# A decoder layer's 64 experts on one core: w1 stored beside w3, two rounding parts in one matmul, blocks of 64 tokens, other groups of tokens

## The chip, the cores and the metric

The kernel runs on one core of a Trainium2 chip. The metric is the device time of one execution in microseconds (us). Before the change it was 3769.25 us, the median of three runs (3760.1 to 3776.89 us).

## What is computed

The reference is one layer of a decoder: a token mixer (RWKV-7, indexer-selected sparse attention and sliding-window attention side by side), then a mixture of experts (MoE). The change touches the second part only. There, 2048 tokens of 1024 numbers are each sent to 8 of 64 experts, and to one shared expert of the same shape:

```python
def swiglu(t, w1, w3, w2):
    return (jax.nn.silu(t @ w1) * (t @ w3)) @ w2
...
    out = grouped_experts(t, idx, gate, w1, w3, w2) + swiglu(t, sw1, sw3, sw2)
```

w1 and w3 are 1024 x 256 and w2 is 256 x 1024, in float32. A token's result is the sum of its 8 experts' outputs, each times the gate of the token for that expert, plus the shared expert's output. A layer norm of that sum with the stream ends the layer.

## The kernel before, in words

**The precision.** TensorE multiplies numbers rounded to its 32-bit matmul type (F32R). To come near float32, each operand is split into a high part (the rounded number) and a low part (the rest), and a product takes three matmuls: high x high, high x low, low x high (`TERMS`, L2017). Every matmul of the experts thus stands three times in the code, and every operand has two tiles. ScalarE (ACT) makes the high part and VectorE (DVE) the low part by a subtraction, for the weights at L1998 and L1999 and for the rest in `split_to` (L58, ACT L61 and DVE L64).

**The units of work.** The experts are ranked by how many tokens chose them; `CAPS` (L1594) has the token capacity of each rank, from 640 down to 128. `group_cuts` (L1603) cuts a capacity into groups of at most 320 tokens. The MoE phase (`moe_phase`, L1953) is a list of units in a fixed order (L2173 to L2181): three units of the shared expert, then the groups of all ranks in the order 0, 63, 1, 62, ..., then the shared expert's other tokens with the last layer norm. There are 82 routed units with 157 blocks of tokens. Their sizes before are 128 or less (21 units), 192 (7), 208 (9), 224 (7), 240 (2), 256 (22), 272 (4), 288 (4), 304 (2) and 320 (4).

**One unit.** `gather` (L2070) fetches the rows of its tokens from memory by indirect DMA on the GpSimd (POOL) queue, one DMA for a block of 128 tokens or what is left. `turn` (L2082) transposes them on TensorE (L2011), eight transposes a block, into the tiles hH and hL. `hidden` (L2019) multiplies by w1 and w3. A unit of more than 128 tokens takes the weights as the stationary operand: for each half m of the 256 hidden columns and for each of w1 and w3 there are 24 matmuls (8 slices k of the 1024 input numbers x 3 terms) of n columns each (L2051), 96 in all. The four sums lie in PSUM tiles of the pool p13, which has three buffers. After each m, silu (ACT L2056), the product (DVE L2057) and a split make gH and gL. A unit of 128 tokens or less takes the tokens as the stationary operand, 48 matmuls of 256 columns (L2032). `back` (L2060) multiplies by w2: for a block and each half of the 1024 output columns six matmuls of 512 columns (L2066), whatever the block's size. `routed` (L2097) scales a result by the gate on ACT (L2102) and adds it to the sums in memory by an indirect DMA (L2103).

**What sets the order.** TensorE's order is written out in the last loop (L2330 to L2371): `hidden` of a unit yields between its matmuls, and `interleave` (L2310) places there the transposes of the next unit and the `back` blocks of the unit before. The rows of tokens are fetched two units ahead, and so are an expert's weights (`matrices`, L2220). A weight goes through four staging buffers of 512 KB (`wraw`, pool wr) on the SP queue, then through ACT L1998 and DVE L1999 into the pool ws. ws has ten tiles and an expert takes six (high and low of w1, w3 and w2), so that a new weight waits until TensorE is done with an old one. The numbers of the tokens (`tokens`, L2124) need a small comparison on DVE (L2119) and a matmul (L2131) first. ACT, DVE, POOL and SP each run their instructions in one fixed order.

Of the kernel before, what the change touches and what calls it, by code (L numbers as in the profile page):

```python
# [13 lines left out]
ALU = mybir.AluOpType  # L14
# [1938 lines left out]
def moe_phase(tc, A, g, S, modrow, out):  # L1953
    nc = tc.nc
    V, G, ACT, PE = nc.vector, nc.gpsimd, nc.scalar, nc.tensor
    with ExitStack() as es:
# [29 lines left out]
        def weights(srcs, into=None, scaled=False):  # L1986

            res = []
            for s in srcs:
                a, b = s.shape[1:]  # L1990
                wh, wl = into or [ws.tile([P, 2048], F32R, name="w") for _ in range(2)]
                for i in range(2):
                    raw = wr.tile([P, 1024], F32, name="wraw")
                    last = nc.sync.dma_start(raw.rearrange("p (a b) -> p a b", b=b), s[:, i * a // 2:(i + 1) * a // 2, :])
                    c = slice(i * 1024, (i + 1) * 1024)
                    if scaled and s is srcs[-1]:
                        V.tensor_tensor(raw, raw, g2b, op=ALU.mult)
                    ACT.activation(wh[:, c], raw, AF.Copy)  # L1998
                    V.tensor_tensor(wl[:, c], raw, wh[:, c].bitcast(F32), op=ALU.subtract)  # L1999
                res.append(tuple(x.rearrange("p (a b) -> p a b", a=a) for x in (wh, wl)))  # L2000
            return res, last

        def expert_matrices(e):
            d = lambda a: a[0][bass.ds(e, 1)].rearrange("o a b -> (o a) b")
            return w13(d(A["exp_w1"])), w13(d(A["exp_w3"])), w2_(d(A["exp_w2"]))
# [13 lines left out]
        def hidden(w, h, n, g_):  # L2019


            hH, hL = h
            gH = gp.tile([P, 2, GMAX], F32R, name="gH")
            gL = gp.tile([P, 2, GMAX], F32R, name="gL")
            g_ += [gH, gL]
            if n <= P:
                ps = []
                for i in range(2):
                    ps.append(p13.tile([P, CH], F32, name="p13"))
                    for k in range(KT):  # L2030
                        for j, (a, b) in enumerate(TERMS):
                            PE.matmul(ps[i][:n, 0:256], lhsT=(hH, hL)[a][:, k, 0:n], rhs=w[i][b][:, k, :],  # L2032
                                      start=(k == 0 and j == 0), stop=(k == KT - 1 and j == 2))
                        if k % STEP == STEP - 1 and (i, k) != (1, KT - 1):
                            yield (2 - i) * (KT // STEP) - k // STEP
                s = gp.tile([P, GMAX], F32, name="s")
                ACT.activation(s[:n, 0:256], ps[0][:n, 0:256], AF.Silu)
                V.tensor_tensor(s[:n, 0:256], s[:n, 0:256], ps[1][:n, 0:256], op=ALU.mult)
# [4 lines left out]
                split_to(nc, gH[:, :, 0:n], gL[:, :, 0:n], pt[:, 0:2 * n].rearrange("p (m t) -> p m t", m=2))  # L2043
                return
            for m in range(2):
                ps = []
                for i in range(2):
                    ps.append(p13.tile([P, CH], F32, name="p13"))
                    for k in range(KT):
                        for j, (a, b) in enumerate(TERMS):  # L2050
                            PE.matmul(ps[i][:, 0:n], lhsT=w[i][a][:, k, m * P:(m + 1) * P], rhs=(hH, hL)[b][:, k, 0:n],  # L2051
                                      start=(k == 0 and j == 0), stop=(k == KT - 1 and j == 2))
# [3 lines left out]
                ACT.activation(s[:, 0:n], ps[0][:, 0:n], AF.Silu)  # L2056
                V.tensor_tensor(s[:, 0:n], s[:, 0:n], ps[1][:, 0:n], op=ALU.mult)  # L2057
                split_to(nc, gH[:, m, 0:n], gL[:, m, 0:n], s[:, 0:n])

        def back(w, gH, gL, c, n):  # L2060
# [355 lines left out]
```

## Time and profile before

| | before |
|---|---|
| median of 3 runs | 3769.25 us |
| the profiled execution's own time | 3762.49 us |
| its span, first to last instruction | 3760.8 us |
| mean granted TensorE clock | 0.964 of full speed |
| experts' stage, routed units with their neighbours | about 2133 to 3630 us of the span |

Views name a group of instructions by line, engine and tile. PE is TensorE's matmuls, PEld its weight loads, which overlap the matmuls. Matmuls overlap in the pipeline, so the time from one start to the next says more than the duration of one. In the chain of waits a piece such as "2.77 PE py L2066 x12" is twelve matmuls that followed each other without a gap, in 2.77 us. "issue" is time for which the profile shows no releaser.

### The profile page before, as it was taken

What the parts mean: (1) busy time and instruction counts of PE and PEld (TensorE: products, weight loads), DVE (VectorE), ACT (ScalarE), POOL (GpSimd) and SP (SyncE); (2) the same over time, 40 slices, a digit from 0 to 9 for tenths busy, and PEclk for the clock granted to TensorE, in tenths of its full rate; (3) what the DMA queues carried; (4) which work ended last, traced back from release to release, by engine and by line L of the source; (5) the groups of instructions that cost most, each with busy time, mean ns of one, the idle gap of its engine ahead of it and who ended that gap; (6) DMA issues with size and microseconds to landing.
All of it is one profiled execution on the core that took longest, in us unless ns stands there. A gap on an engine that the chain in (4) does not pass through costs nothing. (4 is left out here: it accounts for less than half of the span.)

```text
span 3760.8 us, 64004 instructions
## 1 busy us (share of the span) xinstructions
PE 3433.5 (91%) x23044; PEld 2984.6 (79%) x23044; DVE 2670.9 (71%) x7039; ACT 1941.9 (52%) x3439; POOL 883.3 (23%) x817
## 2 busy tenths in 40 slices
PE   7799999799999878999897899999999999999994
PEld 5577777688888767778786799888899888888983
DVE  6556899888888678888799555555665555665669
ACT  4233656355555567766322355555565555556630
POOL 1000000322223255543000122233233223232200
PEclk9899999899999889999998899999999999999997
DMA  7657466400000132222543488888899888888973
GB/s 253 210 192 242 141 216 221 164 27 21 24 24 18 30 107 81 78 69 80 172 149 129 163 213 218 234 237 233 246 266 252 242 223 235 241 248 254 295 226 138
DMA packets 276234, 640.37 MB, mean 170 GB/s; under 512 B 34428, under 2 KB 115364, under 8 KB 275784
## 3 DMA queue, kind: packets, MB, share of 16 engines
q1 hardware_dynamic: 231760, 481.09, 38.1%
q0 software_dynamic: 40832, 150.32, 18.1%
q10 hardware_dynamic: 3320, 4.83, 0.4%
q8 instruction: 182, 2.98, 0.3%
q14 instruction: 140, 1.15, 0.1%
HBM read 467.14 MB, written 169.00 MB: 169 GB/s over the span
## 5 line engine op out<-in xcount | busy, mean ns | idle before, releaser
L2051 PE MATMUL p<-hH,w 128*128 128x256 f32 (+8 forms) x4352 | 872.2, 288 | 9.3 <-DVE w L1999 6.6
L2051 PEld LDWEIGHTS p<-hH,w 128*128 128x128 f32 x4352 | 706.0, 191 | 18.8 <-DVE w L1999 6.9
L1999 DVE TENSOR_TENSOR w<-wraw,w 128x1024 fp32r<-128x1024 f32 x396 | 474.8, 1223 | 285.7 <-ACT w L1998 268.9
L2051 PE MATMUL p<-hL,w 128*128 128x256 f32 (+8 forms) x2176 | 615.9, 283 | 0.7 <-DVE hL L64 0.7
L1998 ACT ACTIVATE w<-wraw 128x1024 fp32r<-128x1024 f32 x396 | 406.1, 1053 | 232.0 <-DMA wraw<-in_exp_w_dram 102.0
L2066 PE MATMUL py<-w,gH 128*128 128x512 f32 (+5 forms) x1384 | 443.8, 403 | 26.2 <-DVE w L2297 14.6
L2103 POOL DMA_INDIRECT scratch_acc<-y,idx x157 | 263.9, 1681 | 797.5 <-ACT y L2102 245.8
L2051 PEld LDWEIGHTS p<-hL,w 128*128 128x128 f32 x2176 | 415.9, 191 | 6.2 <-DVE hL L64 0.9
L285 PE MATMUL pj<-hTH,w 128*128 128x512 f32 x1152 | 379.1, 404 | 21.5 <-ACT w L201 16.4
L64 DVE TENSOR_TENSOR hL<-tr,hH 128x512 fp32r<-128x512 f32 (+7 forms) x346 | 213.0, 626 | 210.9 <-ACT hH L61 192.7
L2066 PEld LDWEIGHTS py<-w,gH 128*128 128x128 f32 (+5 forms) x1384 | 240.5, 182 | 86.7 <-DVE w L2297 15.8
L2102 ACT ACTIVATE y<-py,gt 128x512 f32<-128x512 f32 (+5 forms) x314 | 213.9, 683 | 147.3 <-PE py L2066 131.3
L285 PEld LDWEIGHTS pj<-hTH,w 128*128 128x128 f32 x1152 | 221.9, 194 | 76.0 <-ACT w L201 20.4
L61 ACT ACTIVATE hH<-tr 128x512 fp32r<-128x512 f32 (+7 forms) x346 | 184.0, 544 | 189.6 <-PE tr L2011 165.4
L2066 PE MATMUL py<-w,gL 128*128 128x512 f32 (+5 forms) x692 | 275.9, 399 | 0.3 <-DVE gL L64 0.3
L2077 POOL DMA_INDIRECT x<-scratch_h,idx x157 | 163.5, 1041 | 309.9 <-DVE L L2119 68.5
L285 PE MATMUL pj<-hTL,w 128*128 128x512 f32 x576 | 231.2, 401 | 0.0
L2011 PE MATMUL tr<-ident,x 128*128 128x128 f32 (+5 forms) x1384 | 192.2, 266 | 31.5 <-issue 20.7
L2011 PEld LDWEIGHTS tr<-ident,x 128*128 128x128 f32 (+5 forms) x1384 | 149.8, 141 | 42.7 <-issue 26.0
L2066 PEld LDWEIGHTS py<-w,gL 128*128 128x128 f32 (+5 forms) x692 | 125.2, 181 | 40.0 <-DVE gL L64 1.7
L2032 PE MATMUL p<-w,hH 128*128 128x256 f32 (+2 forms) x736 | 142.6, 291 | 10.7 <-DVE s L2057 10.7
L61 ACT ACTIVATE gH<-s 128x256 fp32r<-128x256 f32 (+8 forms) x136 | 55.1, 405 | 160.4 <-DVE s L2057 147.8
(610 smaller groups left out, 8199.9 us busy)
## 6 DMA issues: line engine op xcount, KB each, us to landing
wraw<-in_exp_w_dram SPq DMA_DIRECT2D x384, 512.0 KB
w<-scratch_wH SPq DMA_DIRECT2D x57, 512.0 KB
w<-scratch_wL SPq DMA_DIRECT2D x57, 512.0 KB
mw<-in_w_mod_dram SPq DMA_DIRECT2D x48, 512.0 KB
scratch_rw<-po SPq DMA_DIRECT2D x44, 256.0 KB
w<-in_w_in_dram SPq DMA_DIRECT2D x21, 512.0 KB
x<-in_x_dram SPq DMA_DIRECT2D x40, 256.0 KB
scratch_wH<-w SPq DMA_DIRECT2D x19, 512.0 KB
```

The source lines that it names most:

```text
L61: nc.scalar.activation(hi, src, AF.Copy)
L64: (lo_eng or nc.vector).tensor_tensor(lo, src, hi.bitcast(F32), op=ALU.subtract)
L285: nc.tensor.matmul(ps, lhsT=a_[:, k, :], rhs=b_[k], start=(k == 0 and i == 0), stop=(k == KT - 1 and i == 2))
L1998: ACT.activation(wh[:, c], raw, AF.Copy)
L1999: V.tensor_tensor(wl[:, c], raw, wh[:, c].bitcast(F32), op=ALU.subtract)
L2011: PE.transpose(ps[:, k * n:(k + 1) * n], x[0:n, (4 * h + k) * P:(4 * h + k + 1) * P], g.ident[0:n, 0:n])
L2032: PE.matmul(ps[i][:n, 0:256], lhsT=(hH, hL)[a][:, k, 0:n], rhs=w[i][b][:, k, :], start=(k == 0 and j == 0), stop=(k == KT - 1 and j == 2))
L2051: PE.matmul(ps[i][:, 0:n], lhsT=w[i][a][:, k, m * P:(m + 1) * P], rhs=(hH, hL)[b][:, k, 0:n], start=(k == 0 and j == 0), stop=(k == KT - 1 ...
L2066: PE.matmul(ps[:n], lhsT=(gH, gL)[a][:, m, c:c + n], rhs=w[2][b][:, m, h * CH:(h + 1) * CH], start=(m == 0 and j == 0), stop=(m == 1 and j ...
L2077: G.indirect_dma_start(out=x[0:m, :], out_offset=None, in_=S["h2"], in_offset=bass.IndirectOffsetOnAxis(ap=ix[0:m], axis=0))
L2102: ACT.activation(y[:m, hs], ps[:m], AF.Copy, scale=gt[:m])
L2103: G.indirect_dma_start(out=S["acc"], out_offset=bass.IndirectOffsetOnAxis(ap=ix[0:m], axis=0), in_=y[0:m, :], in_offset=None, compute_op=A ...
```

## The change

Weights: the two tiles w1 and w3 (high and low of each) become two tiles of another cut. The first holds slices k = 0 to 3 of w1 and of w3 side by side, the second k = 4 to 7. Loads, splits and buffers keep their numbers and sizes, and come in the order w1, w3 of the first tile, w1, w3 of the second.

Units of 128 tokens or less: w1 and w3 go through one matmul of 512 columns, 24 instead of 48 of 256.

Units of 144 to 240 tokens: the tokens' high and low parts lie in one tile hb, and one matmul of 2n columns multiplies both by the high weight; one of n columns adds the low weight. 64 matmuls instead of 96; the two halves of the sum are added afterwards on DVE and ACT.

Blocks: a unit whose last block would have 16 to 64 tokens ends in a block of 64, and the one before is made shorter. In `back` the two parts of 64 tokens make one stationary operand of 128 columns: four matmuls of 512 columns for each output half instead of six. The two halves are added on DVE after a copy on ACT, and the gate is multiplied by a DVE instruction of its own.

Groups: `group_cuts` cuts capacities over 320 in other places. There are still 82 routed units and 157 blocks: 128 tokens (25 units), 192 (6), 208 (2), 224 (8), 240 (6), 256 (17), 272 (5), 288 (6), 304 (3), 320 (4). 24 blocks have 64 tokens.

```diff
@@ group_cuts
     if n <= GMAX:
         return [(0, n)]
-    a = 256
-    if n - a < 192 and 384 < n < 448:
+    if n <= GMAX + P:
+        a = n - P
+    elif n <= 2 * GMAX - 64:
         a = 16 * ((n // 2 + 15) // 16)
+    else:
+        a = 256
     return [(0, a)] + [(a + x, a + y) for x, y in group_cuts(n - a)]
+def blocks_of(n):
+    k, r = divmod(n, P)
+    if k and 0 < r <= 64:
+        cuts = [P] * (k - 1) + [64 + r, 64]
+    else:
+        cuts = [P] * k + [r] * (r > 0)
+    return [(sum(cuts[:i]), m) for i, m in enumerate(cuts)]
...
+        def three(w1, w3, w2, scaled):
+            side = lambda i: lambda t: t.rearrange("p (k i n) -> p k i n", k=4, i=2)[:, :, i, :]
+            half = lambda i: lambda t: t[:, i * 1024:(i + 1) * 1024].rearrange("p (a b) -> p a b", a=1)
+            both = [([(w[:, 4 * q:4 * q + 4, :], side(i)) for i, w in enumerate((w1, w3))], False) for q in range(2)]
+            return both + [([(w2[:, i:i + 1, :], half(i)) for i in range(2)], scaled)]
+        k_of = lambda w, part, k: w[k // 4][part][:, (k % 4) * CH:(k % 4 + 1) * CH]
...
@@ hidden
+            gb = gp.tile([P, 2, 2, 256], F32R, name="gb")
+            gq = gp.tile([P, 2, 2, 64], F32R, name="gq")
+            c, nq = blocks_of(n)[-1]
+            parts = [(gb, 0, c), (gq, c, n)] if nq == 64 and n > P else [(gb, 0, n)]
...
+                ps = p13.tile([P, CH], F32, name="p13")
+                for k in range(KT):
+                    for j, (a, b) in enumerate(TERMS):
+                        PE.matmul(ps[:n], lhsT=hb[:, k, a, 0:n], rhs=k_of(w, b, k),
+                                  start=(k == 0 and j == 0), stop=(k == KT - 1 and j == 2))
...
+            wide = 2 * n <= CH - 32
...
+                        if wide:
+                            two = [(ps[i][:, 0:2 * n].rearrange("p (a t) -> p a t", a=2), wk(0), hb[:, k, :, 0:n]),
+                                   (ps[i][:, 0:n], wk(1), hb[:, k, 0, 0:n])]
+                            for j, (o, l, r) in enumerate(two if k == 0 else two[::-1]):
+                                PE.matmul(o, lhsT=l, rhs=r, start=(k == 0 and j == 0), stop=(k == KT - 1 and j == 1))
...
+                if wide:
+                    s3 = gp.tile([P, 256], F32, name="s3", bufs=1)
+                    V.tensor_copy(s[:, 0:n], ps[0][:, n:2 * n])
+                    V.tensor_tensor(s[:, 0:n], ps[0][:, 0:n], s[:, 0:n], op=ALU.add)
+                    ACT.activation(s3[:, 0:n], ps[1][:, n:2 * n], AF.Copy)
+                    V.tensor_tensor(s3[:, 0:n], ps[1][:, 0:n], s3[:, 0:n], op=ALU.add)
+                    ACT.activation(s[:, 0:n], s[:, 0:n], AF.Silu)
+                    V.tensor_tensor(s[:, 0:n], s[:, 0:n], s3[:, 0:n], op=ALU.mult)
...
-                split_to(nc, gH[:, m, 0:n], gL[:, m, 0:n], s[:, 0:n])
+                for t, a, e in parts:
+                    split_to(nc, t[:, m, 0, 0:e - a], t[:, m, 1, 0:e - a], s[:, a:e])
@@ back
+                    if n == 64:
+                        gq = g_[1][:, m]
+                        two = [(ps, gq.rearrange("p a t -> p (a t)"), w2(0)), (ps[:n], gq[:, 0], w2(1))]
+                        for j, (o, l, r) in enumerate(two if m == 0 else two[::-1]):
+                            PE.matmul(o, lhsT=l, rhs=r, start=(m == 0 and j == 0), stop=(m == 1 and j == 1))
@@ routed
+                    if m == 64:
+                        ACT.activation(y[:m, hs], ps[64:128], AF.Copy)
+                        V.tensor_tensor(y[:m, hs], ps[:m], y[:m, hs], op=ALU.add)
+                    else:
+                        ACT.activation(y[:m, hs], ps[:m], AF.Copy, scale=gt[:m])
+                if m == 64:
+                    V.tensor_scalar(y[:m], y[:m], gt[:m], None, op0=ALU.mult)
```

## Rows read from the trace of the kernel before

**Rows 1.** The page: busy time by engine, and lines of the chain that ended last.

```profile
PE 3433.5 (91%) x23044; PEld 2984.6 (79%) x23044; DVE 2670.9 (71%) x7039; ACT 1941.9 (52%) x3439; POOL 883.3 (23%) x817
...
PE p L2051 18%; PE py L2066 11%; PE tr L2011 3%; PE p L2032 3%; DMA wraw<-in_exp_w_dram 2%; DVE w L1999 1%; ACT w L1998 1%; DVE w L2273 0%; DVE w L2272 0%; DVE lnst L2262 0%; DVE w L2283 0%; DMA scratch_acc<-y,idx 0%; DVE w L2297 0%; DVE hL L64 0%; DVE x L2282 0%
```

**Rows 2.** Busy time in windows of the experts' stage, with clock, DMA share, GB/s.

```profile
2133.00:3630.00 1497.00, 1452.69 (x10444) 1330.45 (x10443) 857.62 (x1931) 840.01 (x1316) 423.44 (x310) 0.99 0.87 243
...
2700.00:2900.00 200.00, 198.11 (x1473) 185.19 (x1472) 122.70 (x287) 116.68 (x182) 63.24 (x44) 1.00 0.91 259
2900.00:3450.00 550.00, 529.24 (x3647) 472.95 (x3647) 320.44 (x735) 313.38 (x492) 161.95 (x121) 0.99 0.86 240
3450.00:3630.00 180.00, 176.06 (x1280) 165.67 (x1279) 104.94 (x189) 99.68 (x155) 40.87 (x29) 0.99 0.94 277
```

**Rows 3.** Waits of TensorE's weight loads, 2120 to 3640: total us, times, longest.

```profile
PEld tr L2011 <- issue: 26.0, 21, 3.4
PEld L2131 <- DVE L L2119: 9.2, 8, 1.3
```

**Rows 4.** The same waits, 2900 to 3450.

```profile
PEld tr L2011 <- issue: 21.1, 17, 3.4
```

**Rows 5.** Chain pieces (start, us, count): columns 192, 224, 256, 272, 288, 304, 320, 512.

```profile
2937.93 1.32 PE p L2051 x12
...
3213.44 1.33 PE p L2051 x12
...
3473.27 1.43 PE p L2051 x12
...
3375.45 3.01 PE p L2051 x24
...
3202.20 3.16 PE p L2051 x24
...
3108.38 3.32 PE p L2051 x24
...
2971.22 3.52 PE p L2051 x24
...
2941.01 2.77 PE py L2066 x12
```

**Rows 6.** DVE and ACT groups, 2120 to 3760: busy, mean ns, idle before and releaser.

```profile
L1999 DVE TENSOR_TENSOR w<-wraw,w 128x1024 fp32r<-128x1024 f32 x386 | 463.0, 1223 | 279.5 <-ACT w L1998 262.7 <-issue 12.0 <-PE py L2066 3.5
L2282 DVE TENSOR_TENSOR x<-x,g2b 128x1024 f32<-128x1024 f32 x16 | 19.3, 1208 | 7.4 <-DMA x<-scratch_acc 7.4
L2297 DVE TENSOR_TENSOR w<-py,w 128x512 f32<-128x512 f32 x20 | 13.4, 670 | 0.5 <-PE py L2066 0.5
L2057 DVE TENSOR_TENSOR s<-s,p 128x224 f32<-128x224 f32 x14 | 5.4, 382 | 4.3 <-PE tr L2011 3.6 <-issue 0.6
...
L2056 ACT ACTIVATE s<-p 128x192 f32<-128x192 f32 x14 | 4.5, 323 | 2.2 <-DVE hL L64 1.4 <-PE p L2051 0.7
```

**Rows 7.** Chain of waits, 2410 to 2460: the end of a 240-token unit.

```profile
2439.54 2.58 PE p L2051 x23
2442.12 0.02 issue
2442.14 1.07 ACT w L1998
...
2444.38 1.22 DVE w L1999
...
2445.70 0.27 DVE L L2119
```

**Rows 8.** Timeline without weight loads, from 2928.65: a transpose that waits (idle in brackets).

```profile
2928.65 1.06 ACT L1998 ACTIVATE w<-wraw 128x1024 fp32r<-128x1024 f32 x1 [2.71 <-DMA wraw<-in_exp_w_dram]
...
2929.74 1.23 DVE L1999 TENSOR_TENSOR w<-wraw,w 128x1024 fp32r<-128x1024 f32 x1 [1.83 <-ACT w L1998]
...
2932.95 0.63 PE L2011 MATMUL tr<-ident,x 128*128 128x128 f32 x4 [2.30 <-issue]
```

**Rows 9.** All waits, 2120 to 3640: total us, times, longest.

```profile
DVE w L1999 <- ACT w L1998: 262.7, 183, 5.4
...
ACT w L1998 <- DMA wraw<-in_exp_w_dram: 99.9, 65, 5.8
```

More of the change, by code (lines that the diff above doesn't have):

```diff
@@ L2019, in hidden @@
         def hidden(w, h, n, g_):
[L2022 to L2025, printed above, removed]
-            if n <= P:
[L2027 to L2035, printed above, removed]
+            hb = h[0]
+            gb = gp.tile([P, 2, 2, 256], F32R, name="gb")
+            gq = gp.tile([P, 2, 2, 64], F32R, name="gq")
+            c, nq = blocks_of(n)[-1]
+            parts = [(gb, 0, c), (gq, c, n)] if nq == 64 and n > P else [(gb, 0, n)]
+            g_ += [gb, gq]
+            if n <= P:
+                ps = p13.tile([P, CH], F32, name="p13")
[3 more added lines that the diff above has]
+                                  start=(k == 0 and j == 0), stop=(k == KT - 1 and j == 2))
+                    if k % 2 and k < KT - 1:
+                        yield 4 - k // 2
                 s = gp.tile([P, GMAX], F32, name="s")
-                ACT.activation(s[:n, 0:256], ps[0][:n, 0:256], AF.Silu)
-                V.tensor_tensor(s[:n, 0:256], s[:n, 0:256], ps[1][:n, 0:256], op=ALU.mult)
+                ACT.activation(s[:n, 0:256], ps[:n, 0:256], AF.Silu)
+                V.tensor_tensor(s[:n, 0:256], s[:n, 0:256], ps[:n, 256:512], op=ALU.mult)
                 yield 1
@@ L2064, in back @@
                 for m in range(2):
-                    for j, (a, b) in enumerate(TERMS):
-                        PE.matmul(ps[:n], lhsT=(gH, gL)[a][:, m, c:c + n], rhs=w[2][b][:, m, h * CH:(h + 1) * CH],
-                                  start=(m == 0 and j == 0), stop=(m == 1 and j == 2))
+                    w2 = lambda part: w[2][part][:, m * 1024 + h * CH:m * 1024 + (h + 1) * CH]
+                    if n == 64:
[3 more added lines that the diff above has]
+                            PE.matmul(o, lhsT=l, rhs=r, start=(m == 0 and j == 0), stop=(m == 1 and j == 1))
+                    else:
+                        for j, (a, b) in enumerate(TERMS):
+                            PE.matmul(ps[:n], lhsT=g_[0][:, m, a, c:c + n], rhs=w2(b),
+                                      start=(m == 0 and j == 0), stop=(m == 1 and j == 2))
                 yield h, ps
@@ L2072, in gather @@
             xs = []
-            for c in range(c0, c0 + n, P):
-                m = min(P, c0 + n - c)
-                ix = idx[c]
+            for c, m in blocks_of(n):
+                ix = idx[c0 + c]
                 x = xg.tile([P, HC], F32, name="x")
@@ L2196, in groups @@
                 numbers(unit)
-                at = [c for c0, c1 in group_cuts(CAPS[r]) for c in range(c0, c1, P)]
+                at = [c0 + c for c0, c1 in group_cuts(CAPS[r]) for c, _ in blocks_of(c1 - c0)]
                 grp[r] = at, beyond_group(cums[r], at)
@@ L2211, in ahead @@
             if r in (None, "s"):
[L2212 removed]
+                for c in range(0, n, P):
                     x = xg.tile([P, HC], F32, name="x")
[L2214 to L2215 removed]
+                    nc.sync.dma_start(x[:, 0:D], S["h2"][c0 + c:c0 + c + P, 0:D])
+                    xs.append((x, P, c))
                 return xs
@@ L2224, in matrices @@
             if r in (None, "s"):
-                src = w13(A["sh_w1"][0]), w13(A["sh_w3"][0]), w2_(A["sh_w2"][0])
+                src = three(w13(A["sh_w1"][0]), w13(A["sh_w3"][0]), w2_(A["sh_w2"][0]), r is None)
             else:
@@ L2229, in matrices @@
             if len(got) < n:
-                more_, la = weights(src[len(got):n], scaled=r is None)
+                more_, la = weights(src[len(got):n])
                 got += more_
@@ L2294, in finish @@
                     under_way.append(norm(r2, sums(r2)))
-                for q, ps in back(w, g_[0], g_[1], c, P):
+                for q, ps in back(w, g_, c, P):
                     hs = slice(q * CH, (q + 1) * CH)
@@ L2304, in begin @@
                 y = yp.tile([P, D], F32, name="y")
-                for q, ps in back(w, g_[0], g_[1], c, P):
+                for q, ps in back(w, g_, c, P):
                     ACT.activation(y[:, q * CH:(q + 1) * CH], ps, AF.Copy)
```

62 lines of the change are left out of this document (30 added, 32 removed).

## The prediction

> **What bounds the kernel now.** I read the page first: TensorE is busy for 91% of the span, and the two experts' lines L2051 and L2066 alone hold 29% of it on the chain that ended last, against 3% for weight transfers and splits together [rows 1]. A share of the whole span says little about one stage, so I cut out the experts' stage by windows. From 2133 to 3630 us PE is busy for 1452.7 of 1497 us at a granted clock of 0.99, near the upper level of 2.4 GHz. Three resources stand close behind: the DMA engines at 0.87, DVE at 858 us (57%) and ACT at 840 us (56%) [rows 2]. Last, the waits: what stops TensorE is mostly transposes (26.0 us in 21 waits) and the matmul that numbers tokens (9.2 us, behind DVE) [rows 3]. Of those 26.0 us, 21.1 fall in the 550 us from 2900 on [rows 4]. So TensorE's issue sets the pace, and a matmul time saved there shortens the stage, unless one of the three resources takes over.
>
> **What the change takes off TensorE.** The unit of account is the time from one matmul's start to the next, from pieces of the chain that ran without a gap [rows 5]: 0.110 us for 192 columns, 0.111 for 224, 0.119 for 256, 0.125 for 272, 0.132 for 288, 0.138 for 304, 0.147 for 320 and 0.231 for 512. From 256 columns up this is a line, 0.435 ns a column plus 8 ns. That line would give 0.091 at 192, but the row has 0.110, the same as at 224. Below 250 columns something else holds a matmul at 0.111, and each matmul has its own weight load.
>
> - Groups. With the old loops, a unit of 192 to 240 tokens costs 96 x 0.111 = 10.65 us, one of 256 11.46, of 272 12.0, of 288 12.7, of 304 13.3, of 320 14.1 and one of 128 48 x 0.119 = 5.73. Over the old list (25, 22, 4, 4, 2, 4 and 21 units) that is 821 us, over the new one (22, 17, 5, 6, 3, 4 and 25) 805: **-16**.
> - Two parts in one matmul. A pair (2n columns, then n) costs the line's value at 2n plus the floor of 0.111, in place of three floors. For n = 192, 208, 224 and 240 the wide one takes 0.175, 0.189, 0.203 and 0.217, so a pair saves 0.047, 0.033, 0.019 and 0.005. With 32 pairs a unit and 6, 2, 8 and 6 such units: 9.0 + 2.1 + 4.9 + 1.0 = **-17**. No row shows a moving operand in two pieces; its bounds are the full gain if it streams like 512 plain columns, and nothing if the pair takes as long as three. I take the first, since 256, 320 and 512 columns lie on one line.
> - w1 beside w3. 24 x 0.231 for 48 x 0.119 is 0.17 us less a unit; 25 routed and two shared units: **-5**. Silu now waits for both sums, some 0.3 us (L2056) [rows 6], hidden by the other units' matmuls; in the very last unit it isn't, and costs that once.
> - Blocks of 64. `back` takes 2 x 6 matmuls of 512 columns for a block of any size; with 64 tokens it will take 2 x 4. Four fewer are 4 x 0.231 = 0.92 us, in 24 blocks: **-22**. This has no unknown but the copy and addition behind it, below.
>
> Sum: -60 us. The transposes stay at eight a block and 157 blocks.
>
> A rule speaks against the second item. The rows give 0.110 us for 192 columns [rows 5]. The Trainium skill's "TensorE: Matmul & The Clock Gate", section Back-to-back issue gap, gives N/2.4 + 2.5 ns for a matmul by itself; by it 192 columns would take 82 ns, two parts in one matmul would save next to nothing, and the sum would be about -43. The measured 0.110 disagrees, and the measurement decides; the same section says that the formula counts too little at small N, where weights must be loaded, and with that the trace agrees.
>
> **What the change adds elsewhere.** Per half m a wide unit gets three more DVE instructions and one ACT copy of n columns: 22 x 2 x 3 x 0.38 = 50 us on DVE, 22 x 2 x 0.32 = 14 on ACT [rows 6]. A block of 64 gets two additions from PSUM at 0.67 and a gate product, for which no row has the shape; half of L2282's 1.21 and all of it bound it, and I take 1.2: 24 x 2.5 = 61 us. The 48 extra splits are under 0.38 us each on DVE, under 0.32 on ACT: 9 and 8 us. DVE gets 858 + 120 = 978 of about 1437 us (68%), ACT 862 (60%), and the DMA engines, with the same bytes, 0.87 x 1497 / 1437 = 0.91. None is full, so this is not a new bound by itself; it costs by delay, because ACT and DVE run in order.
>
> Two places where that shows:
> - At an expert's end a wait runs from the last matmul through a weight split on ACT (1.07) and on DVE (1.22) to the comparison L2119, and TensorE stands before L2131 [rows 7]. A freed weight tile lets that split start. Before, w1's tile was free after three quarters of a unit's matmuls; now both first tiles are read until seven eighths, so more of the splitting falls after the end. At most one more ACT split each, 1.07 us, at some 15 such ends; not below nothing, since no tile is free earlier. I take half: **+8**.
> - Transposes wait for PSUM that ACT and DVE have not emptied, while those stand behind a weight split that waits for its DMA [rows 8]. All told ACT waits 99.9 us for weights and DVE 262.7 for ACT's splits [rows 9]. From 2900 on DVE's load rises from 320 to about 390 us of some 525, from 58 to 74%. If those 21.1 us of waits grow by as much as they have now or not at all, this is 0 to 21 us. I take a little over half: **+12**.
>
> The loads themselves keep sizes, queues and number. SP passes no new wait; the second weight tile is needed after 12 matmuls (1.4 us) rather than 24, and two-ahead loading covers that; without it, 1.2 us an expert.
>
> **Forecast.** -60 + 8 + 12 = -40. The profiled execution has 3762.5 us of its own, so it would become 3722.5. The median of the runs lies 6.8 us above it, which gives **3729 us**.
>
> **Rivals.**
> - *All of it arrives* (15%): DVE's additions fill its idle time and no wait grows. For it: 2700 to 2900 runs with DMA at 0.91, DVE at 61% and PE at 198 of 200 us [rows 2]. 3769 - 60 = 3709.
> - *The wide pair saves nothing* (5%): what holds small matmuls at 0.111 is not the weight load but something that the pair pays as well, so that it takes as long as three. The change then doesn't do what it says in that part: 3729 + 17 = 3746. The flat 0.110 and 0.111 below a straight line [rows 5] speak against it. The formula of the Trainium skill's "TensorE: Matmul & The Clock Gate" would give the same time.
> - *The DMA engines take over* (17%): their 0.87 is an average, with ACT already waiting for weights [rows 9]. If the stage can't go above 0.88, it ends no earlier than 1302 / 0.88 = 1480 us, 17 less than now; with the delays above some 10 are left: 3759. Against it: 0.94 from 3450 on [rows 2] with PE at 176 of 180.
> - *DVE holds the sums* (13%): p13 has three buffers, so a unit's fourth sum reuses the first one's. Until now one ACT instruction emptied that; in a wide unit two DVE instructions do, queued behind weight splits. It decides once DVE lags by more than the two sums between, some 5 us. Behind two splits (2.4) and a mean wait of 262.7 / 183 = 1.4, a unit then loses about 3.9 us. 22 units: +86; with the +8, 3769 - 60 + 94 = **3803**. Against it: interleaved blocks stretch those two sums to near 8 us.
>
> **Numbers.** The forecast has 50%, of which a few points spill over 3750. The runs of before spread over 0.4%, so 0.5%, 19 us, is about what can be told from no change: faster means under 3750, slower over 3788. Faster: 46 + 15 + 5 = 66%; same: 4 + 17 = 21%; slower 13%. The range reaches down past the full gain with a little over (waits that shrink), 3700, and up through the DMA case into the slower one's smaller forms, 3778.
>
> **What would show it.** In the profile after: wide matmuls of 384 to 480 columns that start 0.17 to 0.22 us before the next, and 0.111 for their partners; 96 fewer matmuls of 512 columns in `back`; TensorE's busy time in the stage down by some 60 us; DVE up by 120; waits at transposes and L2131 up by some 20. It is wrong if a wide pair takes 0.33 us, if matmuls of the fourth sum wait for DVE, or if TensorE's waits grow by over 40 us.

## The result and the profile after

The kernel got slower: 3828.47 us in the median of four runs (3814.27 to 3830.86), against 3769.16 before in the same comparison, a ratio of 1.0135 with a 95% interval of 1.0107 to 1.0162. The prediction had 3729. The profiled execution has 3828.91 us, its span, from the first instruction to the last, is 3827.2; that is 66.4 us more than before.

First the page's busy time by engine and the lines of the chain that ended last, beside [rows 1]:

```profile
PE 3434.4 (90%) x21412; PEld 2925.6 (76%) x21412; DVE 2757.8 (72%) x7283; ACT 1966.0 (51%) x3523; POOL 889.2 (23%) x817
...
PE py L2115 4%; DMA wraw<-in_exp_w_dram 4%; PE p L2082 4%; PE p L2079 3%; DVE w L2012 1%; PE tr L2033 1%; ACT w L2011 1%; PE py L2112 1%; DVE w L2326 0%; DVE w L2325 0%; DVE lnst L2315 0%; DVE w L2336 0%; DMA scratch_acc<-y,idx 0%; DVE w L2350 0%; DVE hb L64 0%
```

TensorE has 1632 matmuls fewer and is busy just as long. On the chain the experts' matmuls held 29% and hold 12% now (L2115, L2082, L2079, L2112); the weights' transfers have 4%, 2% before.

Then the experts' stage in windows (columns as in [rows 2]: busy time of each engine, clock, DMA share, GB/s), the first line over the whole stage, 53 us longer than before, the second over the same 550 us as before:

```profile
2144.00:3694.00 1550.00, 1440.49 (x8849) 1262.28 (x8849) 940.97 (x2164) 861.93 (x1399) 428.76 (x310) 0.97 0.85 234
2900.00:3450.00 550.00, 502.62 (x3073) 437.18 (x3072) 359.36 (x872) 312.87 (x532) 159.66 (x120) 0.97 0.84 228
```

TensorE's idle time in the stage was 1497 - 1452.7 = 44 us [rows 2] and is 1550 - 1440.5 = 110: **+65**. Its busy time fell by 12 only. A part of that is the clock. By the trace's clock records, 92 us of TensorE's busy time in the stage lie at the lower of its two levels, 14 before. At half the pace the 78 us more are a loss of some 39 us (the two digits of the clock in the windows, 0.97 and 0.99, give 32). So of the 48 us that are missing from the forecast's 60, some 39 went to matmuls at the lower level; the rest I can't place. The shares of the DMA engines and of ACT are no higher, and DVE has 61% of the stage. The prediction's own sign of being wrong, TensorE's waits up by over 40 us, is there.

What TensorE's weight loads waited for in the stage (total us, times, longest), beside [rows 3]:

```profile
PEld py L2115 <- ACT gb L61: 46.7, 25, 3.5
PEld tr L2033 <- issue: 41.8, 49, 5.1
PEld tr L2033 <- DVE hb L64: 12.1, 7, 3.3
PEld tr L2033 <- DVE tk L2193: 10.5, 7, 3.4
...
PEld L2184 <- DVE L L2172: 8.8, 6, 3.2
PEld tr L2064 <- issue: 7.7, 9, 2.5
```

The first line has no counterpart before: the matmuls by w2 now wait for the hidden numbers (gb) that ACT splits. Transposes (L2033) wait for 41.8 instead of 26.0 at "issue", and for 12.1 and 10.5 on DVE. From the list of all waits, beside [rows 9]:

```profile
DVE w L2012 <- ACT w L2011: 253.6, 148, 5.7
ACT w L2011 <- DMA wraw<-in_exp_w_dram: 132.2, 79, 5.5
```

ACT waits 132.2 us in 79 waits for weights in transit, 99.9 in 65 before. One such stop in the timeline, around an end of a 208-token unit (start, duration, engine and line; in brackets the idle time before and what ended it):

```profile
3213.02 3.90 ACT L2011 ACTIVATE w<-wraw 128x1024 fp32r<-128x1024 f32 x4 [0.33 <-PE p L2079]
...
3214.86 1.36 PE L2079 MATMUL p<-hb,w 128*128 128x208 f32 x8
3215.36 12.30 SPq L2008 DMA_DIRECT2D wraw<-in_exp_w_dram  x6
...
3218.05 0.35 ACT L2091 ACTIVATE s<-p 128x208 f32<-128x208 f32 x1
...
3219.86 0.36 DVE L2092 TENSOR_TENSOR s<-p,s 128x208 f32<-128x208 f32 x1
...
3222.62 1.06 ACT L2011 ACTIVATE w<-wraw 128x1024 fp32r<-128x1024 f32 x1 [4.22 <-DMA wraw<-in_exp_w_dram]
...
3225.30 0.37 ACT L61 ACTIVATE gb<-s 128x208 fp32r<-128x208 f32 x1
...
3225.72 3.91 PE L2115 MATMUL py<-w,gb 128*128 128x512 f32 x9 [3.02 <-ACT gb L61]
```

And the window of those last nine matmuls:

```profile
3225.70:3229.60 3.90, 3.88 (x10) 3.05 (x11) 3.83 (x15) 1.15 (x2) 0.00 (x0) 0.56 0.88 268
```

Read it from the top. Four weight splits run on ACT in one bunch. Each, with DVE's subtraction behind it, frees a staging buffer, so the next loads are issued only from 3215.36 on, and the last sum's eviction (L2091) comes after the bunch. The next split stands on ACT for 4.22 us, waiting for its load. The split of the unit's result, ready for ACT since DVE's product, is queued behind it. TensorE stops for 3.02 us, and its next nine matmuls take 0.434 us each, where 512 columns took 0.231 [rows 5]. The granted clock over them is 0.56, after 1.00 from 3200 to 3220: it has fallen to its lower level.

### The profile page after: what moved, and what is told of

Its sections match the earlier page's. It is cut to its first block, busy times and chain, and to the rows that moved or that the text cites. A ratio compares the mean times of both kernels' runs of the same rounds, so it can differ in the third digit from the quotient of the medians.

```text
span 3827.2 us, 61021 instructions
## 1 busy us (share of the span) xinstructions
PE 3434.4 (90%) x21412; PEld 2925.6 (76%) x21412; DVE 2757.8 (72%) x7283; ACT 1966.0 (51%) x3523; POOL 889.2 (23%) x817
## 5 line engine op out<-in xcount | busy, mean ns | idle before, releaser
L2082 PE MATMUL p<-hb,w 128*128 128x256 f32 (+4 forms) x4032 | 576.6, 296 | 13.8 <-DVE w L2012 6.2
L2082 PEld LDWEIGHTS p<-hb,w 128*128 128x128 f32 x4032 | 538.7, 194 | 24.1 <-DVE w L2012 6.5
L2115 PE MATMUL py<-w,gb 128*128 128x512 f32 (+3 forms) x1788 | 487.6, 419 | 66.2 <-ACT gb L61 36.5
L2115 PEld LDWEIGHTS py<-w,gb 128*128 128x128 f32 (+3 forms) x1788 | 341.4, 197 | 164.1 <-ACT gb L61 47.6
L64 DVE TENSOR_TENSOR hb<-tr,hb 128x512 fp32r<-128x512 f32 (+4 forms) x346 | 215.3, 628 | 160.5 <-ACT hb L61 145.1
L61 ACT ACTIVATE hb<-tr 128x512 fp32r<-128x512 f32 (+4 forms) x346 | 185.0, 545 | 204.6 <-PE tr L2033 185.9
L2079 PE MATMUL p<-hb,w 128*128 128x224 f32 (+7 forms) x1408 | 255.9, 328 | 0.0
L2153 ACT ACTIVATE y<-py,gt 128x512 f32<-128x512 f32 (+3 forms) x266 | 181.3, 684 | 131.1 <-PE py L2115 123.4
L2033 PE MATMUL tr<-ident,x 128*128 128x128 f32 (+4 forms) x1384 | 196.6, 270 | 52.5 <-DVE cj L2192 15.1
L2079 PEld LDWEIGHTS p<-hb,w 128*128 128x128 f32 x1408 | 217.8, 193 | 14.7
L2033 PEld LDWEIGHTS tr<-ident,x 128*128 128x128 f32 (+4 forms) x1384 | 157.1, 143 | 82.2 <-issue 41.8
L2054 PE MATMUL p<-w,hb 128*128 128x512 f32 x648 | 173.0, 402 | 9.6 <-DVE lna L654 9.6
L61 ACT ACTIVATE gb<-s 128x256 fp32r<-128x256 f32 (+4 forms) x128 | 50.0, 390 | 131.8 <-DVE s L2097 102.3
```

Of the source, the lines that this page charges most:

```text
L61: nc.scalar.activation(hi, src, AF.Copy)
L64: (lo_eng or nc.vector).tensor_tensor(lo, src, hi.bitcast(F32), op=ALU.subtract)
L2033: PE.transpose(ps[:, k * n:(k + 1) * n], x[0:n, (4 * h + k) * P:(4 * h + k + 1) * P], g.ident[0:n, 0:n])
L2054: PE.matmul(ps[:n], lhsT=hb[:, k, a, 0:n], rhs=k_of(w, b, k), start=(k == 0 and j == 0), stop=(k == KT - 1 and j == 2))
L2079: PE.matmul(o, lhsT=l, rhs=r, start=(k == 0 and j == 0), stop=(k == KT - 1 and j == 1))
L2082: PE.matmul(ps[i][:, 0:n], lhsT=wk(a), rhs=hb[:, k, b, 0:n], start=(k == 0 and j == 0), stop=(k == KT - 1 and j == 2))
```

## The experiments

The theories changed as the runs came in. The first two were A, the wide units' long end (five instructions on DVE and ACT between a sum and `back`), and B, the blocks of 64. Each run is timed against the kernel before on the same chip. A diff stands against the changed kernel, unless its head names another.

**One part undone.** Wide pairs, blocks of 64, groups, and the evictions' length:

```diff
@@ e1_no_wide
-            wide = 2 * n <= CH - 32
+            wide = False
@@ e2_no_64, blocks_of
-    if k and 0 < r <= 64:
-        cuts = [P] * (k - 1) + [64 + r, 64]
-    else:
-        cuts = [P] * k + [r] * (r > 0)
+    cuts = [P] * k + [r] * (r > 0)
@@ e3_old_groups: group_cuts of before
@@ e4_half_sum
-                    V.tensor_copy(s[:, 0:n], ps[0][:, n:2 * n])
...
+                ACT.activation(s[:, 0:n], ps[0][:, 0:n], AF.Silu)
+                V.tensor_tensor(s[:, 0:n], s[:, 0:n], ps[1][:, 0:n], op=ALU.mult)
```

e4 leaves out the product of the tokens' low part with the high weight in wide units.

> The changed kernel with the wide matmuls undone: units of 192 to 240 tokens take three matmuls of n columns again, with the short end (silu, product, split). All else as changed (3828 us). Theory A, the long end: the six-step end of a wide unit hands work to and fro between DVE and ACT behind weight splits, back waits for it, and the clock falls to half after each stop. Then most of the new stops at back (36 us) and of the low-clock time go with it: about 3755 us, less than 5 us of waits of back for ACT's split, low clock under 40 us in place of 92. Rival B, the blocks of 64 with their longer eviction: 3828 + 17 (matmul time given back) = 3845. Rival C, w1 beside w3 (weight tiles come free later): also 3845. Rival D, the general load of DVE: about 3805.

> The changed kernel with the blocks of 64 undone: blocks of 128 and what is left, six matmuls for each output half, the gate applied on ACT. Wide matmuls, groups and weights as changed. Theory A (long end of wide units): 3828 + 22 = 3850, stops of back unchanged near 36 us. Rival B (blocks of 64): about 3765. Rival C: 3850. Rival D (load of DVE, of which the blocks of 64 add half): about 3800.

> The changed kernel with the groups of before (82 units again, 25 of them wide instead of 22, 21 of 128 tokens or less instead of 25). Theory A: 16 us of matmul time more and three more wide ends, about 3850. If the new order of small units were the cause (rival E): 3770. Rivals B, C and D: about 3844.

> The changed kernel with every matmul of the wide units, but with the end of before: silu and product read the first half of each sum and leave out the second (the tokens' low part times the high weight). TensorE does the same work, and ACT and DVE have four instructions less in each half of a wide unit. Theory A: the stops of back for ACT's split fall below 5 us, and the matmul time saved stays: about 3740. Rivals B and C: the wide end costs nothing, so about 3828. Rival D: about 3805. A separate reading: if the pair of matmuls itself were slow, this would stay near 3828 while e1 falls.

Measured: e1 1.0171 (1.0126 to 1.0217), e2 1.0066 (1.0041 to 1.0091), e3 1.0118 (1.0075 to 1.016), e4 1.0106 (1.0063 to 1.0148), against 1.0135. Theory A falls as the chief cause: without wide pairs the kernel is no faster, and without the long end only 0.3% is seen, less than the intervals. Blocks of 64 cost 0.7% in this company, less than half of what theory B asked of e2 (3765 us, measured 3798.6). The old groups cost nothing that can be told. e1 (3841.0) came near the 3845 us of theories B and C; e3 (3823.1) and e4 (3813.2) lie on none of their forecasts. No run came near 1.0, so w1 beside w3 was left.

**w1 apart, or beside alone.** e5 gives each of w1 and w3 its own tile again and has the rest of the change; e6 is e5 without blocks of 64; e7 is the kernel before with w1 beside w3 alone; e8 is the kernel before with the new groups alone.

```diff
@@ e5_w1_apart, three
-            both = [([(w[:, 4 * q:4 * q + 4, :], side(i)) for i, w in enumerate((w1, w3))], False) for q in range(2)]
+            quart = lambda q: lambda t: t[:, q * 1024:(q + 1) * 1024].rearrange("p (a b) -> p a b", a=4)
+            both = [([(w[:, 4 * q:4 * q + 4, :], quart(q)) for q in range(2)], False) for w in (w1, w3)]
```

> The changed kernel with w1 and w3 in tiles of their own again (loads in the order w1, w3; 48 matmuls of 256 columns in a unit of 128 tokens); wide matmuls, blocks of 64 and groups as changed. Theory C, w1 beside w3: the two tiles are read until the end of a unit, both come free at the same time, and the next weights' splits bunch up on ACT and DVE. Then the ratio to before falls from 1.0135 to about 0.998, TensorE's low-clock time from 92 to under 35 us. Theory F, no single part: everything that shortens TensorE's work is given back by waits for weights: ratio about 1.012, low clock over 60 us. If the blocks of 64 are the one further cause (theory B): 1.013.

> w1 and w3 apart again and blocks of 64 undone; wide matmuls and new groups stay, 33 us of matmul time less than before. Theories B and C together: all that was lost is back, ratio about 0.992. Theory C alone: 0.998. Theory B alone: about 1.005. Theory F: about 1.003.

> The kernel before with w1 beside w3 alone: groups, blocks and three-matmul sums as before (tokens' parts in one tile). Theory C: ratio about 1.012, low clock over 45 us. Theories B and F: 0.999 to 1.002, low clock as before, 14 us.

> The kernel before with the new groups alone: 16 us of matmul time less. Theories B and C: ratio 0.996 to 0.998. Theory F: 1.000 or above, since waits for weights give it back. If the new order of small units costs by itself (rival E): over 1.004.

Measured: e5 1.0042 (1.0028 to 1.0057), e6 0.9986 (0.9968 to 1.0003), e7 **1.0224** (1.019 to 1.0259), e8 **0.9956** (0.9936 to 0.9977). The part that I had priced at -5 us costs 2.2%, 85 us, by itself, and 0.9% in company (e5 against the change). The forecasts of theory C had the direction; e6 lies on its 0.998, e5 misses 0.998, and e7 is at almost twice its 1.2%.

Its timeline in e7, in a stretch where an expert with one unit of 320 tokens and one with a unit of 192 take turns (x24 is the last sum of the 320-token unit; the first row is of the pair of experts before, to show the period):

```profile
3027.78 3.69 PE L2073 MATMUL p<-hb,w 128*128 128x320 f32 x24
...
3078.53 3.90 ACT L2004 ACTIVATE w<-wraw 128x1024 fp32r<-128x1024 f32 x4 [0.46 <-PE py L2106]
3078.56 3.69 PE L2073 MATMUL p<-hb,w 128*128 128x320 f32 x24
...
3080.88 9.68 SPq L2001 DMA_DIRECT2D wraw<-in_exp_w_dram  x6
...
3084.86 1.06 ACT L2004 ACTIVATE w<-wraw 128x1024 fp32r<-128x1024 f32 x1 [1.86 <-DMA wraw<-in_exp_w_dram]
...
3087.88 1.06 ACT L2004 ACTIVATE w<-wraw 128x1024 fp32r<-128x1024 f32 x1 [1.60 <-DMA wraw<-in_exp_w_dram]
3088.84 1.07 ACT L61 ACTIVATE hb<-tr 128x512 fp32r<-128x512 f32 x2
...
3090.36 1.09 PE L2026 MATMUL tr<-ident,x 128*128 128x128 f32 x4 [4.42 <-issue]
```

The same place in the kernel before (its x24 starts at 2971.22 [rows 5]):

```profile
2968.35 2.01 ACT L1998 ACTIVATE w<-wraw 128x1024 fp32r<-128x1024 f32 x2 [1.42 <-PE p L2051]
...
2970.70 9.45 SPq L1994 DMA_DIRECT2D wraw<-in_exp_w_dram  x6
...
2971.15 2.00 ACT L1998 ACTIVATE w<-wraw 128x1024 fp32r<-128x1024 f32 x2
...
2980.24 0.63 PE L2011 MATMUL tr<-ident,x 128*128 128x128 f32 x4 [1.80 <-issue]
```

Ten weight tiles hold five pairs, and an expert takes three. So the splits of the coming weights wait for three returns: the first tile, the second tile, and w2 of the expert before. Before, w1's tile comes back after 3/4 of a unit's matmuls, and two splits run then, two after the next return. Beside each other both tiles are read until late, the first until 7/8; the returns fall together, and four splits run in a row. The six loads that need their staging buffers start at 3080.88, 2.3 us after the last sum's start, where before they started 0.5 us ahead of it; two more splits wait 1.86 and 1.60 us for them. The emptying of the transposes' PSUM (ACT L61, 3088.84) is queued behind, and TensorE stops for 4.42 us.

**Is it the return?** e9 is e7 in which, in the second half m of a unit over 128 tokens, both sums take k 0 to 3 first and then k 4 to 7. The first tile is back at 3/4 again. e10 does so in both halves, so that the second tile is wanted as late as before too; e11 puts e10's order into the whole change.

```diff
@@ e10_halves, hidden (e9: for m == 1 alone)
-                for i in range(2):
-                    ps.append(p13.tile([P, CH], F32, name="p13"))
-                    for k in range(KT):
+                ks = [(i, range(4 * q, 4 * q + 4)) for q in range(2) for i in range(2)]
+                for at, (i, kk) in enumerate(ks):
+                    if len(ps) == i:
+                        ps.append(p13.tile([P, CH], F32, name="p13"))
+                    for k in kk:
@@ e12_groups_64: e5 with wide = False
```

> w1 beside w3 alone, as e7, but in the second half of a unit over 128 tokens (m=1) both sums take k 0 to 3 first, then k 4 to 7, so that the first weight tile is given back after 3/4 of the unit's matmuls, as w1's tile is in the kernel before, instead of after 7/8. The second tile is still needed after 12 matmuls. Theory release (the late and bunched release makes the splits, then the weight loads, then the transposes late): 0.995 to 1.006 of before, the stops before transposes and hidden units back to about the 31 us of before. Rival need (the second tile is wanted after 12 instead of 24 matmuls) and rival layout (strided split writes, one sum of 512 columns): it stays at 1.018 to 1.026.

> As e9, and in the first half of a unit (m=0) too both sums take k 0 to 3 first, so that the second tile is needed after 24 matmuls as before, and the first given back after 3/4. Theory release: about the same as e9, within 0.3%. Rival need: only this one returns to 0.995 to 1.004 and e9 does not. Rival layout: both stay at 1.018 to 1.026.

> The whole change, with e10's order of the k blocks. Theory release: 1.0135 less the 0.8 to 0.9% that w1 beside w3 cost in this company (e5 against the changed kernel) less the 5 us that it saves: 1.001 to 1.006. Need: the same. Layout: stays at 1.010 to 1.016.

> The kernel before with the new groups and the blocks of 64 tokens as one weight, w1 and w3 apart and no wide units. If blocks of 64 cost by themselves (two ACT evictions, two DVE adds and a DVE multiply at each, and one more gathered tile and pair of transposes, at the ends where ACT is late): 1.000 to 1.004, against 0.9956 for groups alone. If they cost only in company with w1 beside w3, 0.988 to 0.996, as their matmuls are 22 us shorter.

Measured: e9 **1.0037** (1.0018 to 1.0057), e10 1.0062 (1.0042 to 1.0081), e11 1.0116 (1.0083 to 1.0149), e12 0.9976 (0.9961 to 0.9991). Of e7's 2.2% the return is 1.9. As causes of e7's loss the rivals fall: e10, which also wants the second tile later, is no better than e9, and the layout is the same in all three. TensorE's weight loads for transposes wait 45.7 us at "issue" in e9, 65.9 in e7, so less, but not the 31 or so that I expected. And e11 misses its range: it gives back only 0.2%, less than the intervals, and lies in the range given to the layout. So in the whole change a second cost stands, and the return's own price there isn't shown. Blocks of 64 by themselves give no 22 us: e12 is 0.2% above e8, within the intervals, and not 0.6% below. (They have no more blocks or transposes, unlike that expectation's bracket; what they add is evictions.)

**The second cost.** In the profile of e11 TensorE waits at the transposes of units up to 128 tokens (L2064), as it never did in the kernel before:

```profile
PE tr L2064 <- DVE s L2060: 9.0, 8, 2.2
```

With one sum of 512 columns, SiLU can't start before both products are complete; before, it ran while the second was summed. e13 is e11 with two sums of 256 columns there. e14 is the kernel before with the new groups and wide pairs in the first half m alone. e15 is the changed kernel again.

```diff
@@ e13_two_sums, hidden, n <= P
-                ps = p13.tile([P, CH], F32, name="p13")
-                for k in range(KT):
+                ps = [p13.tile([P, CH], F32, name="p13") for _ in range(2)]
+                for at, (q, i) in enumerate(((0, 0), (0, 1), (1, 0), (1, 1))):
+                    for k in range(4 * q, 4 * q + 4):
...
-                        PE.matmul(ps[:n], lhsT=hb[:, k, a, 0:n], rhs=k_of(w, b, k),
+                            PE.matmul(ps[i][:n, 0:256], lhsT=hb[:, k, a, 0:n], rhs=k_of(w, b, k)[:, i * 256:(i + 1) * 256],
@@ e14_wide_first (e6)
+                wide = m == 0 and 2 * n <= CH - 32
```

> As e11 (the whole change with the halves of k outer), and units up to 128 tokens keep two sums of 256 columns in the beside layout, k 0 to 3 of both sums first, so that SiLU can run while the second sum goes on. Theory one-sum (with 512 columns SiLU starts only when both are complete, TensorE waits at L2064 for the multiplication, and each such stop costs a stretch at half clock): 1.002 to 1.008, and the waits at L2064 (9.0 us in 8 in e11) below 2. Rival (something that neither form touches): 1.009 to 1.014, whatever L2064 does.

> The kernel before with the new groups and wide pairs in the first half (m=0) of a unit alone; w1 and w3 apart, no blocks of 64. It keeps half of the pairs' matmul saving (about 9 us against e8) but ends a unit as before, without the long chain of evictions. If that chain is what e6 lost against e8 (0.9986 against 0.9956): 0.991 to 0.996, the fastest so far. If the evictions' load on ACT and DVE is what costs: 0.995 to 0.999.

> The changed kernel once more, for a second profile. If the later first scatter (2173.6 us against 2162.5 before) belongs to the change, it comes again within 3 us and the windows of 1000 to 1500 us show a clock of 0.92 again; if it is chance, it comes at 2160 to 2166 with 0.95.

Measured: e13 **1.0015** (0.9998 to 1.0032), 1.0% better than e11 for 5 us more of matmuls; its list of TensorE's waits has no wait at these transposes any more. The 9 us of stops are not the whole 1.0%, 38 us: the granted clock from 2160 to 3600 us is 0.98 in e13 and 0.96 in e11. e13 keeps the weights' layout, so of that rival only its one sum of 512 columns is left, and that is the cost found here. e14 0.9958 (0.9944 to 0.9972), the same as e8: the 9 us of matmul time that its pairs should save don't show. It lies in both of its ranges and so doesn't tell the long end from the load. e15 took 3832.7 us.

e15 was for 11 of the 66 us, which are lost ahead of the stage, in code that the change doesn't touch. The windows of 1000 to 1500 us, before, changed and e15:

```profile
1000.00:1500.00 500.00, 436.34 (x3521) 377.79 (x3519) 407.55 (x1096) 306.77 (x706) 175.03 (x195) 0.95 0.16 48
...
1000.00:1500.00 500.00, 437.33 (x3480) 379.74 (x3479) 401.99 (x1082) 300.73 (x695) 169.56 (x187) 0.92 0.16 48
...
1000.00:1500.00 500.00, 436.96 (x3489) 379.38 (x3488) 402.05 (x1084) 302.45 (x697) 171.27 (x189) 0.93 0.16 48
```

The granted clock is lower there in both profiles of the changed kernel, and the first addition to the sums in memory comes at 2173.9 and 2179.1 us instead of 2162.8, so neither of e15's forecasts (again within 3 us, or at 2160 to 2166) came. e14, faster than before, has it at 2177.6, and e9 at 2159.0. In ten of all twenty profiles it lies between 2157 and 2167, in ten between 2173 and 2181. Late are nine of the eleven profiles with w1 beside w3, and of the nine without only e14. That speaks for the kernel; but there is one profile of each other kernel, no path is known, and it stays open whether chance has a part.

**Does an earlier return gain?** If the return sets the time, a tile given back sooner than in the kernel before must make it faster. In e16 to e18 units over 128 tokens take w1 for both halves m, then w3 for both: w1's tile is back at 1/2, and the first sums' evictions lie under w3's matmuls. e16 has the new groups alone, e17 all of the change but w1 beside w3, e18 that without blocks of 64.

```diff
@@ hidden, n > P (e17, e18 on e5 and e6)
-            for m in range(2):
-                ps = []
-                for i in range(2):
-                    ps.append(p13.tile([P, CH], F32, name="p13"))
+            s = [gp.tile([P, GMAX], F32, name="s") for _ in range(2)]
+            for at, (i, m) in enumerate(((0, 0), (0, 1), (1, 0), (1, 1))):
+                ps = p13.tile([P, CH], F32, name="p13")
...
+                elif i == 0:
+                    ACT.activation(s[m][:, 0:n], ps[:, 0:n], AF.Silu)
...
+                else:
+                    V.tensor_tensor(s[m][:, 0:n], s[m][:, 0:n], ps[:, 0:n], op=ALU.mult)
```

> The kernel before with the new groups alone (as e8), and units over 128 tokens take w1 for both halves first, then w3 for both: w1's tile is given back after 1/2 of the unit instead of 3/4, w3's is needed after 1/2 instead of 1/4. Theory release in general: 0.986 to 0.994. Rival (3/4 was early enough): 0.9936 to 0.998, as e8.

> The whole change with w1 apart (as e5, 1.0042), in e16's order; the first sums' evictions (DVE copy, DVE add, SiLU) lie under w3's matmuls. Theory release in general: 0.985 to 0.997, the waits of L2116 (the back matmuls) for ACT's gb under half of e5's 15.9 us. Rival: 1.001 to 1.007.

> As e17 without blocks of 64 (as e6, 0.9986). Theory release in general: 0.983 to 0.993, the fastest. Rival: 0.996 to 1.000.

Measured: e16 0.9907 (0.9872 to 0.9942), e17 **0.986** (0.9832 to 0.9888, 3720.48 us in the median), e18 0.9865 (0.9836 to 0.9893). The rival falls clearly in e17 and e18; in e16 the interval just reaches into its range. One thing was not separated: w3 is also wanted later, after 1/2 of the unit. But the list of TensorE's waits in the kernel before has no matmul of L2051 that waits for a weight, so there was nothing to gain there that a trace shows. A pair of the same sizes in e16 (x24 again the last sum of the 320-token unit):

```profile
2986.44 3.69 PE L2077 MATMUL p<-hb,w 128*128 128x320 f32 x24
...
3030.81 2.01 ACT L2008 ACTIVATE w<-wraw 128x1024 fp32r<-128x1024 f32 x2 [0.46 <-PE py L2112]
...
3030.84 3.69 PE L2077 MATMUL p<-hb,w 128*128 128x320 f32 x24
...
3034.42 1.06 ACT L2008 ACTIVATE w<-wraw 128x1024 fp32r<-128x1024 f32 x1 [1.02 <-PE p L2077]
...
3036.69 1.06 ACT L61 ACTIVATE hb<-tr 128x512 fp32r<-128x512 f32 x2
...
3038.72 0.63 PE L2029 MATMUL tr<-ident,x 128*128 128x128 f32 x4 [0.49 <-PE p L2077]
```

No split waits for its load here, and the transposes wait for 0.49 us. From one x24 to the next it is 44.4 us, in e7 50.8; in the kernel before it is 47.8 (from L2131 at 2926.80, behind one such sum, to L2131 at 2974.59, behind the next). ACT's wait for weights in transit over the stage, first e7, then e9, e16, e17 and e5 ([rows 9] has 99.9 before):

```profile
ACT w L2004 <- DMA wraw<-in_exp_w_dram: 115.9, 74, 4.3
...
ACT w L2004 <- DMA wraw<-in_exp_w_dram: 97.7, 62, 3.8
...
ACT w L2008 <- DMA wraw<-in_exp_w_dram: 25.1, 17, 3.6
...
ACT w L2011 <- DMA wraw<-in_exp_w_dram: 31.3, 24, 3.3
...
ACT w L2011 <- DMA wraw<-in_exp_w_dram: 139.5, 72, 5.4
```

With w1 back at 1/2 this wait all but goes. It doesn't rank the other kernels: e5, with w1 back at 3/4, has more of it than the changed kernel (132.2) and is 0.9% faster.

## Why the prediction was wrong, point by point

**The matmuls were right.** Pieces of the chain, beside [rows 5]: eight matmuls (four pairs) for 192 and for 208 tokens, 32 for 224, and eight of a block of 64:

```profile
2924.79 1.15 PE p L2079 x8
...
3164.45 1.21 PE p L2079 x8
...
2903.32 5.02 PE p L2079 x32
...
2901.46 1.86 PE py L2112 x8
```

A pair takes 0.288, 0.303 and 0.314 us; predicted were 0.175 + 0.111 = 0.286, 0.300 and 0.314. The moving operand in two pieces streams like plain columns, and the rival "the wide pair saves nothing" is out. A block of 64 takes 0.232 a matmul, predicted 0.231. Of the prediction's readings one is off: transfers and splits together have 4% of the chain in [rows 1], not 3%; nothing rests on it.

**Groups, -16.** e8 shows 0.0044 of 3776, some 17 us (9 to 24 by its interval). Right by itself; in the changed kernel it doesn't show (e3 against the change).

**The load on DVE and ACT.** Predicted were 978 and 862 us; the windows show 941 and 862. DVE's estimate was high, in part by the gate product: put at 1.2 and in truth 0.74, in 24 blocks 11 us. The groups of DVE (columns as in [rows 6]), for a block of 64 and a wide unit's copy:

```profile
L2151 DVE TENSOR_TENSOR y<-py,y 64x512 f32<-64x512 f32 x48 | 31.6, 678 | 22.2 <-ACT y L2150 21.9 <-issue 0.3
...
L2155 DVE TENSOR_SCALAR y<-y,gt 64x1024 f32<-64x1024 f32 x24 | 17.7, 738 | 0.1
...
L2089 DVE COPY s<-p 128x224 f32<-128x224 f32 x16 | 6.2, 386 | 9.9 <-PE p L2079 9.9
```

**The step that failed** is the expert's end, "At most one more ACT split each, 1.07 us, at some 15 such ends", taken as +8, with the sentence that "SP passes no new wait". It saw the right event, w1's tile free at seven eighths instead of three quarters, and then priced one split at one place. The late return doesn't add a split, it bunches what was spread: splits, then the staging buffers they free, then the loads, then splits that wait on ACT for a load with evictions behind them. TensorE's stop in e7 was 4.42 us where before it was 1.80, and the clock falls behind it. e7 against e9 prices it at 1.9% by itself, some 70 us for a term of 8. The sentence on SP holds for the totals: its queue waits 861 us for DVE's subtractions, which free the staging buffers, in the kernel before, and 845 in the changed one. What moved is when a wait ends: in e7 the loads start 2.8 us later against the last sum than before.

In the changed kernel this step and the cost called hidden, below, are shown together: with both undone (e13) 1.2% come back, 45 us of the 99 that the forecast was off. The other half is a step at the prediction's start, "a matmul time saved there shortens the stage, unless one of the three resources takes over": none took over, and with the old order of w1 and w3 the savings of the pairs and of the blocks of 64 still don't arrive. With w1 back at 1/2 the kernel is at 0.986 (e17), and the forecast was 0.989.

**w1 beside w3, -5.** Its matmuls are saved, and alone it costs 85 us (e7), by the step above and the next.

**A cost called hidden.** "Silu now waits for both sums, some 0.3 us (L2056) [rows 6], hidden by the other units' matmuls": it isn't hidden, because SiLU, product and transposes follow in a row. e11 against e13 prices it at 1.0%, with the stops' clock.

**The transposes, +12.** In the changed kernel their waits at "issue" grew by 16 us [rows 3], inside the 0 to 21 that I gave. But all waits of L2033 together, those for DVE's hb and tk with them, grew from 35 to 68 us, by 32: the term was too small.

The 46.7 us before the matmuls by w2 were in no step. I took them for the wide units' long end, but e4, which leaves that end out, still has 45.6. Without wide pairs (e1) or without blocks of 64 (e2) most of them go; here e1, e2 and e4:

```profile
PEld py L2115 <- ACT gb L61: 12.4, 13, 1.6
...
PEld py L2110 <- ACT gb L61: 13.0, 9, 4.0
...
PEld py L2106 <- ACT gb L61: 45.6, 27, 4.5
```

With the early return (e11) they are 13.9. So they need the pairs, the blocks of 64 and the late return at once; by what path isn't shown. Nor are they the loss itself: e1 and e11 have few of them and stand at 1.0171 and 1.0116.

**Two parts in one matmul, -17.** TensorE saves them, but with the old order of w1 and w3 the kernel gets 0.3% slower (e6 against e8); with w1 back at 1/2 it gets 0.4% faster, 16 us (e18 against e16). In both comparisons the intervals overlap.

**Blocks of 64, -22.** "This has no unknown but the copy and addition" was too sure. With w1 back at 3/4 and no wide pairs they cost 0.2%, less than the intervals (e12 against e8); beside wide pairs they cost 0.6 to 0.7%, clear of them (e5 against e6, the change against e2). With w1 back at 1/2 (e17, e18) they are worth nothing that can be told. Why the four matmuls saved are not seen I haven't tried.

**The rivals.** None was it. The slower one, DVE holding p13's sums, gave 3803, but no wait of the fourth sum for DVE stands among TensorE's large ones. "The DMA engines take over" put the limit at 0.88; the share was 0.85 in the slower kernel, and e17 ran its stage with more:

```profile
2120.00:3580.00 1460.00, 1413.67 (x9555) 1283.52 (x9556) 951.86 (x2193) 862.41 (x1412) 441.39 (x311) 0.99 0.90 251
```

With the return at 1/2 and without w1 beside w3, the change gains 1.4%, 53 us, and beats both kernels (e17). The order by itself is worth 0.5% (e16 against e8, intervals that overlap), in company 1.8% (e17 against e5).

## What to carry to other kernels

Before moving a buffer's last reader later, list everything that its return starts, down to the next load and the engine queue that the load's consumer heads: the price is not one instruction but a queue in order standing for a transfer. Where weights stream through few tiles, order the loops so that one tile is done with early (all uses of w1, then all of w3); in this company that gained more than any part that saved matmuls. And merging two sums into one also merges their ends: look at what used to run under the second.

## What the runs showed of the hardware that was not expected

A stop of TensorE costs more than itself: after 3.02 us of waiting, nine matmuls of 512 columns took 3.91 us, 0.434 each against 0.231, and over the stage TensorE was busy for 92 us at the lower level instead of 14, some 39 us of pace. A 64x1024 multiplication by one number a row took 0.74 us on DVE, where the 128x1024 product of two tiles takes 1.21 (L2282) [rows 6]. The Trainium skill's "VectorE: DVE Perf Modes", section The perf-mode tier table, says that float32 operations on one tensor in SBUF can run at twice the rate of those on two; the two rows agree in direction, at 1.6 times, though they differ in partitions too. The estimate of 1.2 came from a row of two tensors.
